# Three mixer parts of 256, 256 and 512 tokens, one token tile moved between the dense and the gathered expert pass, and 1-KB gate runs

## The chip, the cores and the metric

The kernel runs on one core of one Trainium2 chip. The metric is the device time of one execution in microseconds (us). Five engines work side by side: TensorE (PE, with its weight loads shown apart as PEld), VectorE (DVE), ScalarE (ACT), GpSimd (POOL, which issues the indirect DMAs) and SyncE (SP, which issues most other DMAs). All DMAs share 16 DMA engines.

## The reference

One layer of a decoder, 1024 tokens of width 1024, all in float32:

```python
h = rms_norm(x, norm_mix_g);  proj = h @ w_in
x = x + concat([diff_attention(...), mlstm(...)]) @ w_out        # the mixer, causal
# PEER: per token 8 heads x 16 experts out of 16384
xb = rms_norm(x, norm_ffn_g)
q = xb @ w_query;  s = einsum(q, sub_keys)                       # 2 x 128 scores per head
eidx, top_s = product_top_k(top_k(s, 16))                        # second top-k, 16 of 256 sums
g = softmax(top_s)
a = gelu(einsum('td,thkd->thk', xb, expert_u[eidx]))
x = x + einsum('thk,thkd->td', g * a, expert_v[eidx])
x = x + sigmoid(rms_norm(x, norm_ple_g) @ w_ple_gate) * (p @ w_ple_proj)
out = rms_norm(x, final_norm_g)
```

## The kernel before

The 1024 tokens are eight tiles of 128. A float32 product is made of three fp32r matmuls (high by high, high by low, low by high), so each weight block is split on the chip into a high half (ACT) and a low half (DVE). PE issues these from `mm3s`, line L143.

**Front** (`front(part, ptk)`, L220). It runs twice, for tiles 0 to 3 and 4 to 7 (T = 512 columns, NT = 4 tiles). Each part streams 29 blocks of `w_in` (4 heads of 7, and the gates), 8 of `w_out` and 16 of `w_query`, each 512 KB, through `weight` (L190: DMA, ACT L195, DVE L196; three raw buffers, two split ones). A block of `w_in` or `w_query` feeds 24 matmuls of N = T columns. Around them lie attention, mLSTM, the norm, and the first top-k (L595 to L604).

**Experts.** Tiles 4 to 7 (`DORD`, 512 tokens) go the dense way, tiles 0 to 3 (`NS` = 4) the sparse way.
- `dense_up` (L818): for each of 128 blocks j of `expert_u`, load and split it (`table`, L753 and L754), 24 matmuls of N = 512 against the normed activations that the second part left in SBUF, Gelu into `ga` (L866), and a store to DRAM `ga_s`. Beside it `gate_blocks` (L764) spreads the chosen softmax weights into a dense gate table in DRAM, `g_s`, in 32 pieces (PE L806, L807). The second top-k of the part run last is called from here (`late`).
- `dense_down` (L879): for each of 128 blocks of `expert_v`, split it (L753, L754 again), multiply `ga` by the gate (L915), split (L916, L917) and 24 matmuls of N = 512 into eight PSUM banks (`keep`). `gq` (the gate, runs of 4 j x 32 tokens x 4 B = 512 B) and `aq` (the activations) come back from DRAM in groups of GC = 4 blocks.
- `sparse` (L704): one step gathers 128 rows of `expert_u`, one per token (512 KB, L700 into `ru`), dots them with the activations on DVE (L716), gathers 128 rows of `expert_v` (`rv`) and adds them with their weight to `ya` (DVE L734). There are 128 such pairs per tile; the v half runs 16 steps behind. `ring["bufs"]` buffers of each kind are in flight: 4 at first, 8 in `dense_down`, 2 from block FLUSH = 108.

**Order.** The sparse work is a generator. `pump(x)` (L212) adds x to a debt and takes that many steps from it, at a scheduling priority 800 instructions lower; the front pumps only in part 1 (`F_RATE * part`), then `dense_up` at 1.5 and 1.6 steps per block and `dense_down` at 1.6, and `tail` 8 twice per tile. The generator is topk2 of tiles 0 and 1, topk2 of tiles 2 and 3 (14 yields each), then the steps of tiles 0 to 3. Each queue keeps the order fixed at build time. In part 1 the loads of x stand on POOL's queue (L235, L251).

**Tail** (`tail`, L956): per tile the last norm, gate and projection (48 and 12 matmuls of N = 512), in the order 4, 0, 5, 1, 6, 2, 7, 3. For tiles 0 to 3 it first reads `x3_s`, which `sparse` writes when the tile is done (L738, L969).

Of the kernel before, what the change touches and what calls it, by code (L numbers as in the profile page):

```python
# [24 lines left out]
NPART = S // T  # L25
# [13 lines left out]
NS = 4  # L39
NDT = S // P - NS  # L40
TD = NDT * P
DORD = list(range(NT, 2 * NT)) + list(range(NS, NT))
NX = 2 * P if NDT > NT else 0
CH1 = T - (NX - (NDT - NT) * P) if NDT > NT else T
GC = 4
GQB = 2
VBF = 4
# [23 lines left out]
F_RATE = (2.4, 1.6, 2.0)  # L71
UP_RATE = (1.5, 1.6, 56)
DOWN_RATE = 1.6
# [3 lines left out]
def layer(ctx, tc, x, xT, pT, gcols, grows, win, convw, convb, gbias, lams, wout, wq, subk,  # L77
          wple, wproj, eu, ev, ut, vr, ident_d, maskneg_d, maskpos_d, tri_d, sel_d, bl_d, br_d, iota_d, out):
# [18 lines left out]
    gcol = load_const(gcols, [P, 21], "gcol")  # L97
    ident = const.tile([P, P], F32, name="ident")
# [8 lines left out]
    ga_s = dram.tile([P, P, TD], F32, name="ga_s")  # L107
# [38 lines left out]
    def bcast_rows(pool, psum, cols, name):  # L146
        ps = psum.tile([P, NT, P], F32, name="tr")
        for i in range(NT):
            pe.matmul(ps[:, i, :], cols[:, i:i + 1].to_broadcast([P, P]), ident,
                      start=True, stop=True)  # L150
        r = pool.tile([P, T], F32, name=name)
# [3 lines left out]
    eidx, gsm, sel_i, fcs = {}, {}, {}, {}  # L155
# [64 lines left out]
    def front(part, ptk):  # L220
        t0 = part * NT
        with ExitStack() as c1:
# [5 lines left out]
            with pool(f"pa{part}", bufs=1) as pa:  # L228
# [3 lines left out]
                for dc in range(DC):  # L232
                    if dc % 2 == 0:
                        x2t = pa.tile([P, 2, T], F32, name="p", bufs=3)
                        (gp if part else sy).dma_start(x2t, xT[part, :, dc:dc + 2, :])  # L235
# [21 lines left out]
                def project(blk):  # L257
                    pump(F_RATE[0] * part)
# [71 lines left out]
                for h in range(H):  # L330
# [5 lines left out]
                    if part:  # L336
                        sy.dma_start(kT[:, :T], kt_s[h])
                        sy.dma_start(vv[:, :NT, :], v_s[h])
                    ps = project(h * 7 + 1)
                    v.tensor_tensor(kT[:, part * T:(part + 1) * T], ps, rb, op=OP.mult)  # L340
                    ps = project(h * 7 + 2)
                    by_tile(vv[:, t0:t0 + NT, :], token_major(ps), lambda i: r1[:, i:i + 1])
                    if part < NPART - 1:
                        sy.dma_start(kt_s[h], kT[:, :T])
                        sy.dma_start(v_s[h], vv[:, :NT, :])
# [3 lines left out]
                    for i in range(NT):  # L349
# [39 lines left out]
                        jb = pa.tile([P, P], BF16, name="jb", bufs=2)  # L389
# [95 lines left out]
                    for i in range(NT):  # L485
                        jb = pa.tile([P, P], BF16, name="jb", bufs=2)
# [17 lines left out]
            with pool(f"pb{part}", bufs=1) as pb_:  # L504
# [13 lines left out]
                for blk in range(2):  # L518
                    pss = [sps.tile([P, 2, 512], F32, name="S") for _ in range(2)]
                    for q in range(4):  # L520
                        pump(F_RATE[2] * part)
# [30 lines left out]
                for i in range(NT):  # L552
                    if t0 + i < NS or t0 + i in DORD[CH1 // P:]:
# [15 lines left out]
                for hc in range(2):  # L569
                    pump(F_RATE[1] * part)  # L570
                    pair.append((*weight(wp, wq[hc], [DC, P]), mmp.tile([P, T], F32, name="mm")))
                for cs in (slice(0, T // 2), slice(T // 2, T)):
# [568 lines left out]
```

## Time and profile before

| | us |
|---|---|
| median of 3 runs (3245.26 to 3264.1) | 3249.8 |
| profiled execution | 3289.41 |
| its span, first to last instruction | 3287.6 |
| PE, DVE, ACT, POOL busy in it | 2711.8, 2651.6, 1046.9, 1372.9 |

The span is what the rows describe; the profiled execution's own time holds 1.8 us around it. Busy time of an engine is the union of its instructions; a chain of back-to-back instructions overlaps, so that the distance from start to start is shorter than the duration of one. The number of the mean granted clock is a share of TensorE's 2.4 GHz.

### The profile page before, as it was taken

What the parts mean: (1) busy time and instruction counts of PE and PEld (TensorE: products, weight loads), DVE (VectorE), ACT (ScalarE), POOL (GpSimd) and SP (SyncE); (2) the same over time, 40 slices, a digit from 0 to 9 for tenths busy, and PEclk for the clock granted to TensorE, in tenths of its full rate; (3) what the DMA queues carried; (4) which work ended last, traced back from release to release, by engine and by line L of the source; (5) the groups of instructions that cost most, each with busy time, mean ns of one, the idle gap of its engine ahead of it and who ended that gap; (6) DMA issues with size and microseconds to landing.
All of it is one profiled execution on the core that took longest, in us unless ns stands there. A gap on an engine that the chain in (4) does not pass through costs nothing.

```text
span 3287.6 us, 37409 instructions
## 1 busy us (share of the span) xinstructions
PE 2711.8 (82%) x12348; PEld 2143.1 (65%) x12348; DVE 2651.6 (81%) x5837; ACT 1046.9 (32%) x1755; POOL 1372.9 (42%) x1044
## 2 busy tenths in 40 slices
PE   8999889999989986999899996878888887827602
PEld 6777766576777765787787875666666666615401
DVE  5555697788899999887998987778888787998863
ACT  4445333344422323343344432222222222203200
POOL 0000000133332554655565674465555556674561
PEclk9999997799999996999999998989998988968856
DMA  3113431355674987999999999999999999997873
GB/s 137 65 63 107 143 120 38 119 188 183 237 260 151 350 311 272 380 377 371 366 412 367 413 408 370 351 371 352 359 360 362 339 383 371 389 336 271 265 258 119
DMA packets 326467, 911.85 MB, mean 277 GB/s; under 512 B 28480, under 2 KB 101056, under 8 KB 324224
## 3 DMA queue, kind: packets, MB, share of 16 engines
q0 software_dynamic: 149760, 545.33, 45.0%
q1 hardware_dynamic: 158080, 330.57, 27.9%
q10 hardware_dynamic: 18432, 33.56, 2.7%
q8 instruction: 97, 1.59, 0.2%
q14 instruction: 98, 0.80, 0.1%
HBM read 827.56 MB, written 81.79 MB: 277 GB/s over the span
## 4 chain that ended last, share of the span: by engine, by line
PE 37%; DMA 20%; DVE 18%; issue 16%; POOL 7%; ACT 2%; DVEq 0%; POOLq 0%; SPq 0%; ACTq 0%
PE mm L143 13%; PE A L143 9%; DMA raw<-in_vr 7%; DMA ru<-in_eu,eidx 5%; DMA rv<-in_ev,eidx 5%; DVE ya L734 4%; POOL rv L700 3%; POOL ru L700 3%; PE S L359 3%; DVE ru L716 3%; PE S L143 2%; DVE tlo L754 2%; PE tr L387 1%; PE pg L807 1%; PE pg L806 1%
## 5 line engine op out<-in xcount | busy, mean ns | idle before, releaser
L700 POOL DMA_INDIRECT ru<-in_eu,eidx x512 | 673.2, 1315 | 869.8 <-DVE ru L716 441.3
L700 POOL DMA_INDIRECT rv<-in_ev,eidx x512 | 690.6, 1349 | 507.9 <-DVE ya L734 304.0
L734 DVE SCALAR_TENSOR_TENSOR ya<-rv,cf,ya 128x1024 f32<-128x1024 f32 x512 | 657.0, 1283 | 101.7 <-DMA rv<-in_ev,eidx 78.6
L716 DVE SCALAR_TENSOR_TENSOR ru<-ru,sh 128x1024 f32<-128x1024 f32 x512 | 624.1, 1220 | 41.9 <-DMA ru<-in_eu,eidx 37.1
L753 ACT ACTIVATE thi<-raw 128x1024 fp32r<-128x1024 f32 x256 | 271.5, 1061 | 921.4 <-DMA raw<-in_vr 510.3
L143 PE MATMUL A<-ahi,thi 128*128 128x512 f32 x1024 | 408.0, 398 | 11.7 <-ACT ga L866 6.4
L754 DVE TENSOR_TENSOR tlo<-raw,thi 128x1024 fp32r<-128x1024 f32 x256 | 312.3, 1220 | 122.0 <-ACT thi L753 112.0
L143 PE MATMUL A<-alo,thi 128*128 128x512 f32 x1024 | 404.2, 395 | 0.0
L143 PE MATMUL keep<-thi,ph 128*128 128x512 f32 x1024 | 284.3, 424 | 144.6 <-ACT ph L916 75.7
L143 PEld LDWEIGHTS keep<-thi,ph 128*128 128x128 f32 x1024 | 207.4, 205 | 201.3 <-ACT ph L916 81.1
L143 PE MATMUL mm<-ahi,whi 128*128 128x512 f32 (+1 forms) x752 | 302.1, 406 | 17.4 <-ACT ahi L237 9.2
L143 PE MATMUL mm<-alo,whi 128*128 128x512 f32 (+1 forms) x752 | 292.5, 402 | 6.7 <-DVE alo L238 6.7
L143 PE MATMUL keep<-tlo,ph 128*128 128x512 f32 x1024 | 267.8, 406 | 20.4 <-DVE tlo L754 20.1
L143 PE MATMUL A<-ahi,tlo 128*128 128x512 f32 x1024 | 263.9, 401 | 23.9 <-DVE tlo L754 23.8
L143 PE MATMUL keep<-thi,pl 128*128 128x512 f32 x1024 | 256.9, 394 | 6.3 <-DVE pl L917 6.3
L143 PEld LDWEIGHTS keep<-tlo,ph 128*128 128x128 f32 x1024 | 203.6, 200 | 68.5 <-DVE tlo L754 23.7
L143 PEld LDWEIGHTS A<-ahi,tlo 128*128 128x128 f32 x1024 | 196.3, 193 | 70.5 <-DVE tlo L754 29.7
L143 PEld LDWEIGHTS A<-ahi,thi 128*128 128x128 f32 x1024 | 195.7, 191 | 57.9 <-ACT ga L866 12.1
L143 PEld LDWEIGHTS keep<-thi,pl 128*128 128x128 f32 x1024 | 195.0, 191 | 47.9 <-DVE pl L917 6.7
L143 PEld LDWEIGHTS A<-alo,thi 128*128 128x128 f32 x1024 | 195.6, 191 | 39.5
L143 PE MATMUL mm<-ahi,wlo 128*128 128x512 f32 (+1 forms) x752 | 196.0, 391 | 2.8 <-DVE wlo L196 2.8
L196 DVE TENSOR_TENSOR wlo<-wraw,whi 128x1024 fp32r<-128x1024 f32 x106 | 129.1, 1218 | 58.7 <-ACT whi L195 44.1
(436 smaller groups left out, 4149.2 us busy)
## 6 DMA issues: line engine op xcount, KB each, us to landing
raw<-in_ut SPq DMA_DIRECT2D x128, 512.0 KB, 7.0
raw<-in_vr SPq DMA_DIRECT2D x128, 512.0 KB, 7.8
ga_s<-ga ACTq DMA_DIRECT2D x128, 256.0 KB, 6.6
g_s<-st SPq DMA_DIRECT2D x16, 2048.0 KB, 10.4
gq<-g_s SPq DMA_DIRECT2D x32, 1024.0 KB, 9.9
aq<-ga_s SPq DMA_DIRECT2D x32, 1024.0 KB, 12.2
wraw<-in_win SPq DMA_DIRECT2D x58, 512.0 KB, 3.4
wraw<-in_wq SPq DMA_DIRECT2D x32, 512.0 KB, 4.1
```

The lines of the kernel that those rows point to most:

```text
L143: pe.matmul(o, ll if p == "l" else lh, rl if p == "r" else rh, start=start and p == "h", stop=stop and n == last and p == names[-1])
L196: anchor(v.tensor_sub(lo.rearrange("p a b -> p (a b)"), raw, hi.rearrange("p a b -> p (a b)").bitcast(F32)))
L359: pe.matmul(sp_[:, n0:n1], qT[64 * c:64 * c + 64, i * P:(i + 1) * P], kT[64 * c:64 * c + 64, n0:n1], start=True, stop=False)
L387: pe.matmul(po, wT[:, kt, :], vv[:, kt, :], start=kt == 0, stop=kt == g)
L700: gp.indirect_dma_start(out=b, out_offset=None, in_=table, in_offset=bass.IndirectOffsetOnAxis(ap=eidx[part][:, i, k:k + 1], axis=0))
L716: behind(v.scalar_tensor_tensor(b, b, 1.0, st["h", tl], op0=OP.mult, op1=OP.mult, accum_out=st["d", n][:, j:j + 1]))
L734: op = v.scalar_tensor_tensor(ya, b, st["c", n][:, j:j + 1], ya, op0=OP.mult, op1=OP.add)
L753: sc.activation(hi, raw, AF.Copy)
L754: anchor(v.tensor_sub(lo, raw, hi.bitcast(F32)))
L806: pe.matmul(pg[:, b, :], o0[:, a, :, b], w0[:, a, :, b], start=True, stop=False)
L807: pe.matmul(pg[:, b, :], o0[:, a, :, b], w1[:, a, :, b], start=False, stop=True)
```

## The change

The front runs three times: tiles 0 and 1, tiles 2 and 3 (256 columns each), tiles 4 to 7 (512). Every part streams all 53 weight blocks. The generator starts after the first part: topk2 of tiles 0 and 1, sparse of tiles 0 and 1, topk2 of tiles 2 and 3, sparse of tile 2. Tile 3 leaves `sparse`. It joins tiles 4 to 7 in `dense_up`, which now works on 640 columns (384 of the part in SBUF, and 256 of tiles 7 and 3 that are loaded from `h2_s` and transposed), and its activations go to `ga_s` with rows of 640. In `dense_down` the new generator `middle` fetches tile 3's 128 chosen activations per token out of `ga_s`, one number per token by an indirect DMA, multiplies them by the softmax weights, gathers the rows of `expert_v` and adds them up. `gq` is loaded for GQ = 8 blocks at a time (runs of 8 x 32 x 4 B = 1 KB). The pump rates differ.

```diff
-NPART = S // T
+PARTS = ((0, 2), (2, 2), (4, 4))
+NPART = len(PARTS)
-NS = 4
-NDT = S // P - NS
+NS = 3
+DORD = list(range(NT, 2 * NT))
+MID = [3]
+UORD = DORD + MID
+NDT = len(DORD)
 TD = NDT * P
+TU = len(UORD) * P
+NX = 2 * P
+CH1 = TU - NX
+GQ = 8
-F_RATE = (2.4, 1.6, 2.0)
-UP_RATE = (1.5, 1.6, 56)
-DOWN_RATE = 1.6
+F_RATE = ((0.0, 0.0, 0.0), (1.0, 0.8, 1.0), (2.4, 1.6, 2.0))
+UP_RATE = (1.8, 2.0, 56)
+DOWN_RATE = 1.05
...
-    ga_s = dram.tile([P, P, TD], F32, name="ga_s")
+    ga_s = dram.tile([P, P, TU], F32, name="ga_s")
...
     def front(part, ptk):
-        t0 = part * NT
+        t0, NT = PARTS[part]
+        T = NT * P
...
-                        jb = pa.tile([P, P], BF16, name="jb", bufs=2)
+                        jb = pa.tile([P, P], BF16, name="jb", bufs=1)
...
-                    if t0 + i < NS or t0 + i in DORD[CH1 // P:]:
+                    if t0 + i < NS or t0 + i in UORD[CH1 // P:]:
...
+            for n, tl in enumerate(UORD):
+                if tl in MID and t0 + tg <= tl < t0 + tg + TG:
+                    i = tl - t0
+                    aidx[tl] = sp.tile([P, PH * K], I32, name=f"aidx{tl}")
+                    own[tl] = sp.tile([P, PH * K], F32, name=f"own{tl}")
+                    v.scalar_tensor_tensor(own[tl], i1a[:, i, :], 128.0, i0a[:, i, :], op0=OP.mult, op1=OP.add)
+                    v.tensor_scalar(aidx[tl], own[tl], float(TU), colp[:, n:n + 1], op0=OP.mult, op1=OP.add)
...
+    def middle(tiles, rs):
+        flat = ga_s.rearrange("j i t -> (j i t)")[:, None]
+        units = [(tl, k0) for tl in tiles for k0 in range(0, PH * K, K)]
+        ya = {}
+
+        def value(n, j):
+            tl, k = units[n][0], units[n][1] + j
+            gp.indirect_dma_start(out=own[tl][:, k:k + 1], out_offset=None, in_=flat,
+                                  in_offset=bass.IndirectOffsetOnAxis(ap=aidx[tl][:, k:k + 1], axis=0))
+
+        for n in range(len(units) + 1):
+            if n > 0:
+                tl, k0 = units[n - 1]
+                part, i = LOC[tl]
+                cf = rs.tile([P, K], F32, name="cf", bufs=2)
+                v.tensor_tensor(cf, own[tl][:, k0:k0 + K], gsm[part][:, i, k0:k0 + K], op=OP.mult)
+                if k0 == 0:
+                    ya[tl] = rs.tile([P, D], F32, name="ya", bufs=1)
+                    gp.dma_start(ya[tl], x2_s[tl])
+            for j in range(K):
+                if n < len(units):
+                    value(n, j)
+                if n > 0:
+                    b = gather(k0 + j, tl, ev, "ru" if j % 2 else "rv")
+                    behind(v.scalar_tensor_tensor(ya[tl], b, cf[:, j:j + 1], ya[tl], op0=OP.mult, op1=OP.add))
+                    if j % 2 == 0:
+                        continue
+                yield True
+            if n > 0 and k0 + K == PH * K:
+                sy.dma_start(x3_s[tl], ya[tl])
+                stored.add(tl)
...
-            it = gp_.tile([P, 4, P], F16, name="it", bufs=2)
+            it = gp_.tile([P, 4, P], F16, name="it", bufs=1)
...
-            late = chain(lambda: topk2(1, ptk, [0, 2]))
+            late = chain(lambda: topk2(2, ptk, [0, 2]))
...
-                    gq, aq = gtiles(g0 // GC)
-                    sy.dma_start(gq, g_s[:, :, g0:g0 + GC, :].rearrange("b i j t -> i b (j t)"))
-                    sy.dma_start(aq, ga_s[g0:g0 + GC].rearrange("j i t -> i j t"))
+                    if g0 % GQ == 0:
+                        gq = mp.tile([P, P // GB * NDT, GQ, GB], F32, name="gq", bufs=GQB)
+                        sy.dma_start(gq, g_s[:, :, g0:g0 + GQ, :].rearrange("b i j t -> i b (j t)"))
+                    aq = gtiles(g0 // GC)
+                    sy.dma_start(aq, ga_s[g0:g0 + GC, :, :TD].rearrange("j i t -> i j t"))
...
-    pumped["gen"] = chain(lambda: topk2(0, ptk, [0]), lambda: topk2(0, ptk, [2]),
-                          lambda: sparse(range(NS), rs))
-    front(1, ptk)
+    pumped["gen"] = chain(lambda: topk2(0, ptk, [0]), lambda: sparse(range(2), rs), lambda: topk2(1, ptk, [0]),
+                          lambda: sparse(range(2, NS), rs))
+    for part in range(1, NPART):
+        front(part, ptk)
...
+    pumped["gen"] = chain(*([lambda g=pumped["gen"]: g] if pumped["gen"] else []), lambda: middle(MID, rs))
     dense_down(yac)
```

## Rows read from the trace of the kernel before

**Rows 1.** The page: the span, the busy time of each engine, and the span in 40 slices (tenths busy, granted clock in tenths, DMA share in tenths, GB/s).

```profile
span 3287.6 us, 37409 instructions
PE 2711.8 (82%) x12348; PEld 2143.1 (65%) x12348; DVE 2651.6 (81%) x5837; ACT 1046.9 (32%) x1755; POOL 1372.9 (42%) x1044
PE   8999889999989986999899996878888887827602
DVE  5555697788899999887998987778888787998863
PEclk9999997799999996999999998989998988968856
DMA  3113431355674987999999999999999999997873
```

**Rows 2.** Busy time by stretch (windows): length of the stretch, busy us (instructions) of each engine, granted clock, DMA share, GB/s. The stretches are front part 0, front part 1, the first 31 blocks of dense_up, the rest of it, dense_down, and the tail; their bounds are in rows 3.

```profile
0.00:470.00 470.00, 435.95 (x2169) 340.82 (x2169) 291.88 (x1182) 210.00 (x480) 3.04 (x9) 0.97 0.29 101
470.00:1048.00 578.00, 540.37 (x2447) 391.58 (x2447) 495.02 (x1772) 223.16 (x486) 144.75 (x120) 0.89 0.50 169
1048.00:1300.00 252.00, 204.64 (x927) 164.50 (x928) 250.31 (x732) 78.44 (x94) 127.39 (x93) 0.88 0.83 303
1300.00:1977.00 677.00, 642.82 (x3190) 535.71 (x3189) 593.66 (x677) 266.67 (x309) 406.66 (x294) 0.97 0.98 384
1977.00:2897.00 920.00, 752.37 (x3072) 606.04 (x3072) 732.77 (x940) 206.78 (x269) 498.37 (x377) 0.91 0.99 364
2897.00:3288.00 391.00, 135.62 (x544) 104.46 (x544) 288.01 (x539) 61.88 (x119) 192.71 (x154) 0.66 0.72 244
```

**Rows 3.** Single lines of the program within front part 0, front part 1, or the whole span: count, shortest, median and longest duration in ns, start of the first and of the last one. L586 is the end of a query block (16 per part), L333 the first use of a head's first projection (4 per part), L866 the Gelu of dense_up, L929 the first work after dense_down.

```profile
L586 ACT ACTIVATE qq<-mm x16: 597/598/600, 368.8 to 464.5; 128x512 f32<-128x512 f32 x16
L333 DVE SCALAR_TENSOR_TENSOR qT<-mm,rb x4: 676/682/686, 497.0 to 786.6; 128x512 f32<-128x512 f32 x4
L586 ACT ACTIVATE qq<-mm x16: 597/598/602, 947.1 to 1047.9; 128x512 f32<-128x512 f32 x16
L866 ACT ACTIVATE ga<-A x128: 575/598/648, 1060.6 to 1977.3; 128x512 f32<-128x512 f32 x128
L929 DVE TENSOR_TENSOR yac<-keep,yac x8: 674/674/679, 2896.6 to 2901.9; 128x512 f32<-128x512 f32 x8
```

**Rows 4.** The timeline of PE: start, length, what. Two of 16 matmuls of 256 columns that follow one another, two of 16 of 512 columns, and two of 30 gate matmuls.

```profile
365.77 0.28 PE L143 MATMUL mm<-ahi,whi 128*128 128x256 f32 x1
...
367.54 0.28 PE L143 MATMUL mm<-ahi,wlo 128*128 128x256 f32 x1
...
1718.58 0.39 PE L143 MATMUL A<-ahi,thi 128*128 128x512 f32 x1
...
1721.98 0.39 PE L143 MATMUL A<-alo,thi 128*128 128x512 f32 x1
...
1724.03 0.29 PE L806 MATMUL pg<-w,o 128*128 128x128 f16 x1
...
1727.45 0.30 PE L807 MATMUL pg<-w,o 128*128 128x128 f16 x1
```

**Rows 5.** The same stretches for line L716 alone, the dot of a sparse step: two instructions (the product and the reading of its sum) per step.

```profile
470.00:1048.00 578.00, 76.02 (x124) 0.89 0.50 169
1048.00:1300.00 252.00, 56.14 (x92) 0.88 0.83 303
1300.00:1977.00 677.00, 181.79 (x295) 0.97 0.98 384
1977.00:2897.00 920.00, 220.82 (x362) 0.91 0.99 364
2897.00:3288.00 391.00, 93.48 (x152) 0.66 0.72 244
```

**Rows 6.** The timeline of DVE where steps follow one another without a wait.

```profile
2910.78 1.24 DVE L716 SCALAR_TENSOR_TENSOR ru<-ru,sh 128x1024 f32<-128x1024 f32 x1
...
2913.18 1.21 DVE L716 SCALAR_TENSOR_TENSOR ru<-ru,sh 128x1024 f32<-128x1024 f32 x1
```

**Rows 7.** DMA queues in the stretch 1300 to 1977, and the stores of the activations: packets, MB, share of 16 engines (q0 is what POOL issues, q1 SP, q10 ACT); for an issue its count, KB each, us to landing.

```profile
q0 software_dynamic: 42404, 154.41, 58.6%
q1 hardware_dynamic: 16091, 79.83, 29.3%
q10 hardware_dynamic: 13968, 25.43, 9.9%
ga_s<-ga ACTq DMA_DIRECT2D x97, 256.0 KB, 6.7
```

**Rows 8.** The same for the stretch 1977 to 2897.

```profile
q0 software_dynamic: 54034, 196.74, 55.5%
q1 hardware_dynamic: 101989, 137.25, 43.4%
ru<-in_eu,eidx POOLq DMA_INDIRECT x187, 8.9
rv<-in_ev,eidx POOLq DMA_INDIRECT x186, 8.9
```

**Rows 9.** Who waited for whom, over the whole span: us in total, times, longest.

```profile
ACT thi L753 <- DMA raw<-in_vr: 510.3, 106, 20.1
POOL ru L700 <- DVE ru L716: 441.3, 128, 21.8
PE tr L984 <- DMA x<-x_s: 146.6, 1, 146.6
```

**Rows 10.** The weight stream of the front, from the page: the low half's split, and the loads (KB each, us to landing).

```profile
L196 DVE TENSOR_TENSOR wlo<-wraw,whi 128x1024 fp32r<-128x1024 f32 x106 | 129.1, 1218 | 58.7 <-ACT whi L195 44.1
wraw<-in_win SPq DMA_DIRECT2D x58, 512.0 KB, 3.4
```

**Rows 11.** The end of the timeline: the last store of a sparse tile, its reload, and the first and one of the last instructions that use it.

```profile
3253.21 0.33 SPq L738 DMA_DIRECT2D x_s<-ya  x1
3255.88 0.33 SPq L969 DMA_DIRECT2D x<-x_s  x1
3259.10 1.97 PE L984 MATMUL tr<-ident,x 128*128 128x128 f32 x8 [146.60 <-DMA x<-x_s]
...
3275.97 1.27 ACT L1017 ACTIVATE gt<-acc,hr 128x512 f32<-128x512 f32 x2 [4.41 <-PE acc L143]
```

**Rows 12.** The slice of the front with the lowest granted clock among windows of 80 us, columns as in rows 2.

```profile
480.00:560.00 80.00, 77.09 (x274) 46.34 (x274) 57.38 (x318) 29.91 (x59) 1.05 (x2) 0.76 0.17 56
```

More of the change, by code (lines that the diff above doesn't have):

```diff
@@ L24 @@
 NT = T // P
-NPART = S // T
+PARTS = ((0, 2), (2, 2), (4, 4))
+NPART = len(PARTS)
+LOC = {t0 + i: (n, i) for n, (t0, nt) in enumerate(PARTS) for i in range(nt)}
 DC = D // P
@@ L146, in bcast_rows @@
     def bcast_rows(pool, psum, cols, name):
-        ps = psum.tile([P, NT, P], F32, name="tr")
-        for i in range(NT):
+        nt = cols.shape[-1]
+        ps = psum.tile([P, nt, P], F32, name="tr")
+        for i in range(nt):
             pe.matmul(ps[:, i, :], cols[:, i:i + 1].to_broadcast([P, P]), ident,
                       start=True, stop=True)
-        r = pool.tile([P, T], F32, name=name)
+        r = pool.tile([P, nt * P], F32, name=name)
         sc.activation(r, ps.rearrange("p a b -> p (a b)"), AF.Copy)
         return r
-    eidx, gsm, sel_i, fcs = {}, {}, {}, {}
+    eidx, gsm, sel_i, fcs, aidx = {}, {}, {}, {}, {}
+    own = {}
     def front_consts(fc):
@@ L220, in front @@
     def front(part, ptk):
-        t0 = part * NT
+        t0, NT = PARTS[part]
+        T = NT * P
+        xT_ = xT[:, t0 * DC * P:(t0 + NT) * DC * P].rearrange("p (c t) -> p c t", c=DC)
+        f_rate = F_RATE[part]
         with ExitStack() as c1:
@@ L518, in front @@
                 for blk in range(2):
-                    pss = [sps.tile([P, 2, 512], F32, name="S") for _ in range(2)]
+                    pss = [sps.tile([P, 2, 512], F32, name="S") for _ in range(NT // 2)]
                     for q in range(4):
-                        pump(F_RATE[2] * part)
+                        pump(f_rate[2])
                         hi, lo = weight(wp, wout[blk, q], [2, 512])
@@ L569, in front @@
                 for hc in range(2):
-                    pump(F_RATE[1] * part)
+                    pump(f_rate[1])
                     pair.append((*weight(wp, wq[hc], [DC, P]), mmp.tile([P, T], F32, name="mm")))
-                for cs in (slice(0, T // 2), slice(T // 2, T)):
+                for cs in (slice(0, T // 2), slice(T // 2, T)) if T > 256 else (slice(0, T),):
                     for a in pair:
@@ L580, in front @@
                     else:
-                        pump(F_RATE[1] * part)
+                        pump(f_rate[1])
                         hi, lo = weight(wp, wq[hc], [DC, P])
@@ L608, in topk2 @@
         sv, sfa = fcs["sv", part]
-        t0 = part * NT
+        t0, NT = PARTS[part]
         if part in gsm:
@@ L615, in topk2 @@
         sel_i[part], gsm[part] = (i0a, i1a), gsa
-        if t0 < NS:
+        if t0 < NS or any(t0 <= tl < t0 + NT for tl in MID):
             eidx[part] = sp.tile([P, NT, PH * K], I32, name=f"eidx{part}")
@@ L621, in topk2b @@
         sv, sfa = fcs["sv", part]
-        t0 = part * NT
+        t0, NT = PARTS[part]
         i0a, i1a = sel_i[part]
@@ L720, in coef @@
             tl, k0 = units[n]
-            part, i = divmod(tl, NT)
+            part, i = LOC[tl]
             cf = rs.tile([P, K], F32, name="cf", bufs=2)
@@ L770, in gate_blocks @@
         for n, tl in enumerate(DORD):
-            part, i = divmod(tl, NT)
+            part, i = LOC[tl]
             fl = gp_.tile([P, 3, P], F32, name="fl", bufs=1)
@@ L963, in tail @@
             for tl in TORD:
-                part, i = divmod(tl, NT)
-                if tl < NS:
+                part, i = LOC[tl]
+                if tl not in DORD:
                     while tl not in stored:
@@ L1113, in layouts @@
         iota_d=np.arange(P, dtype=f),
+        colp_d=np.arange(TU, dtype=f).reshape(len(UORD), P).T,
         ident_d=np.eye(P, dtype=f),
```

46 lines of the change are left out of this document (22 added, 24 removed).

## The prediction

> **What bounds the kernel now.** I read the page first [rows 1]: no engine is above 82% over the span, and the digits change from stretch to stretch, so the average says nothing. The DMA digits are 1 to 5 in the first third and 9 from slice 19 to 36; PE falls to 0 near the end. Then the windows by stage [rows 2], cut at the ends of the stages [rows 3].
> - Front part 0, 470 us: PE 436 busy at clock 0.97, DVE 292, DMA 0.29. PE is the bound and nothing is gathered.
> - Front part 1, 578 us: PE 540, DVE 495.
> - dense_up: first 252 us DVE, 250 busy. Then 677 us in which PE is 643 busy and DMA 0.98: the two are about even.
> - dense_down, 920 us: DMA 0.99, PE 752. The split of the table waits 510 us for its raw block [rows 9], so DMA is the bound.
> - Tail, 391 us: PE works 136. It waits 147 us in one piece for the last sparse tile [rows 9], which is stored at 3253 and reloaded [rows 11].
>
> So transfers are short of room late and have plenty early, and the sparse tiles are finished too late.
>
> **Prices.** From start to start [rows 4], 15 intervals each: a matmul of 256 columns takes 1.77 / 15 = 0.118 us, of 512 columns 3.40 / 15 = 0.227; a gate matmul 3.42 / 29 = 0.118. No matmul of 384 columns is in the trace: it lies between 0.118 and 0.227, and I take the middle, 0.172, because the two rows grow with the columns. A sparse step (u and v) takes DVE 2913.18 - 2910.78 = 2.40 us [rows 6]. A gather takes all DMA engines 0.555 x 920 / 373 = 1.37 us [rows 8].
>
> **Front, parts 0 and 1: 470 becomes 590.** Before, 45 blocks of `w_in` and `w_query` and 8 of `w_out` give 53 x 24 x 0.227 = 288 us of L143; the other 182 are small matmuls and chains. Two half parts: 2 x 45 x 24 x 0.118 = 255, `w_out` 44 (its columns are weights, so its count halves with the tiles), together 299; the 182 divide over the tiles. New: a second start, from the last query block to the first head, 497.0 - 464.5 = 32 us [rows 3]. Weight supply: a half-width block gives PE only 24 x 0.118 = 2.83 us, while its raw block lands in 3.4 and its low half takes DVE 1.22 [rows 10]. Two split and three raw buffers hide most of it. The bounds are 0 and 3.4 + 1.22 - 2.83 = 1.8 us per block, that is 0 to 190 us over 106 blocks; I take 0.45, 47 us, since buffers overlap the loads. Part 1 pumps 49.8 yields (29 x 1.0 + 8 x 1.0 + 16 x 0.8), of which some 25 run there: 25 x 2.4 = 60 us of DVE, beside a DVE that was busy 62% in part 0; half on the path, 30 (0 to 60). Sum 299 + 182 + 32 + 47 + 30 = 590.
>
> **Part 2: 578 becomes 592.** Its 28 yields of second top-k are gone (one pair of tiles is now in part 1, one in dense_up). Before, 83 steps were pumped (111 yields less 28) and 124 / 2 = 62 ran [rows 5], 21 behind. After, 161 - 14 = 147 are pumped by its end; 21 behind is 126, some 20 of them in part 1. DVE: 495, less 54 pairs x 2.4 = 130, less at most 73 for the top-k (495 - 292 - 130), plus 106 x 2.4 = 254, is 546. PE's 540 stays, so both are near full: 592 (578 to 640). The loads of x for this part now stand behind gathers on POOL's queue; its longest wait for a ring buffer is 22 us [rows 9], so 0 to 22, which is inside that range.
>
> **dense_up: 929 becomes 1120.** PE per block: 24 x (0.172 + 0.118) = 6.97 against 5.44. The second stretch holds 97 blocks [rows 7]; PE's floor there was 97 x 5.44 + 873 x 0.118 (L806, L807) = 631 of 677, 93%. After: 97 x 6.97 + 103 = 779, over 0.93 = 838. The first stretch is DVE's: 0.3 more steps in 31 blocks, 22 us, on 252, plus the transposes of the two reloaded tiles (16, under 10 us): 282. Together 1120. Others beside it: DMA was 0.83 x 252 + 0.98 x 677 = 873 us. Steps run: 378 - 126 = 252, less the half-filled ends, 470 gathers against 385 [rows 2, 5], so + 116, and the wider `ga_s` rows add a quarter of 0.099 x 677 = 67, 17: 1006 of 1120. DVE: 844, plus 58 more steps and one more top-k (14 yields) at 2.4, 173: 1017. All three are near full. The ends are PE's floor, 128 x 6.97 + 122 = 1014, and all at the first stretch's pace, 1190.
>
> **dense_down: 920 becomes 760.** After dense_up 38 sparse steps are left, some 64 gathers, and `middle` adds 128 of `expert_v`: 192 x 1.37 = 263 us against 511. The rest of its DMA was 0.434 x 920 = 399. Runs of 512 B are slower: q1 moved 137 MB at 0.434 here and 80 MB at 0.293 x 677 in the stretch without `gq`, that is 21.5 against 25.2 bytes per ns and engine. All of the 59 us that this costs is the most that longer runs can give back; half the number of runs, I take 25. The 128 small gathers move a thousandth of the bytes: I take 10, between 0 and a full gather's 175. Sum 263 + 374 + 10 = 647. PE's floor 128 x 5.44 = 696, over 0.93 = 748, plus 12 for the first load, which is now twice as long: 760. PE becomes the bound here; with the small gathers at their upper end DMA would be (812, at 0.99 about 820). `cf` waits on DVE for sixteen small gathers, and the split of the next table block queues behind it. They are issued a unit ahead, so nothing; without that lead, eight landings of 8.9 us [rows 8], 71.
>
> **Tail: 391 becomes 160.** `middle` needs 80 yields after those 38; 1.05 x 128 = 134 are pumped. At the end of dense_down before, 459 were pumped and 436 run. A lag of 23 leaves some 8 yields for the tail, and tile 3 is last in its order. PE's work: 384 + 96 matmuls x 0.227 and 64 transposes, together 125; the first evacuation 5, the chain after the last gate 12 [rows 11], and 18 for the six weight blocks still to be split: 160 (140 to 200).
>
> **At nothing:** `jb` and `it` with one buffer are written and read in order by one engine (ACT, DVE), and no wait in the trace names them; if DVE and ACT were apart there, 0.4 us x 32. The extra `h2` store goes to SP behind the weight loads, once.
>
> **Sum.** 590 + 592 + 1120 + 760 + 160 = 3222 against 470 + 578 + 929 + 920 + 391 = 3288, with 1.8 around it 3224 against the profiled 3289.41. The median stands at 3249.8 / 3289.41 = 0.988 of that execution: **3185**.
>
> **The rivals.**
> - **Half-width blocks starve PE (slower).** If weights come late in parts 0 and 1, PE idles between blocks and its granted clock falls, as in the slice after the start of part 1: 0.76, between the levels of 2.4 and 1.2 GHz [rows 12]. The 481 us of PE's path then become 481 x 0.97 / 0.76 = 614: + 133, 3355 in the span, 3315. It decides against the change from 66 us on, a mean clock of 0.85. For it: 2.83 us of work under a 3.4-us load. Against it: part 0 holds 0.97 at an unbroken stream, and three raw buffers.
>  The Trainium skill (TensorE: Matmul & The Clock Gate, "HAM oscillation — how this bites in real kernels") warns of just this: where a tile's matmuls are shorter than the wait for the next load, the clock drops in every tile. Taken in full, at 1.2 GHz throughout both parts, that would be an estimate of some 3630; the trace has no slice of 80 us in the front below 0.76, so it bears out only the milder form.
> - **The backlog runs in the front (no change).** If the 21 steps that I leave behind run within part 2's query blocks, they cost 21 x 2.4 = 50 us there, and dense_up, bound by PE, gives nothing back: 3235.
> - **It doesn't start earlier.** The scheduler may leave the pumped steps of parts 1 and 2 behind, as it did with a quarter of them: with 80 done instead of 126, 92 gathers move on, 126 us of DMA, of which dense_up (114 free) and dense_down (113 free) take most; some 40 stay: 3225.
> - **Larger gain.** Parts 0 and 1 at 512 (no stall), dense_up at 1070 and dense_down at 730: 158 us less, half of it at once likely: 3105.
>
> **How the numbers follow.** Forecast 0.53, starving 0.21, backlog 0.12, no earlier start 0.05, larger gain 0.09. A difference below about 0.5% can't be told from no change here. Faster than 3234: most of the forecast and all of the last, part of the middle ones, 0.62; within 0.5%: 0.16; slower: the first rival and a little more, 0.22. The range reaches to the larger gain and to the milder starving: 3090 to 3310; the forecast's own is 3120 to 3240.
>
> **What would show it.** Right: last query block of the second part near 590 and of the third near 1180 at a clock of 0.9 or more; matmuls of 384 columns 0.17 us apart; dense_up about 1120 long with PE over 90% busy; in dense_down no long waits for `in_vr`; no wait of the tail for `x3_s`; tile 3's store before the tail's last tile. Wrong: a clock near 0.76 before 590, a dense_up beyond 1190, or a tail that still waits.

## The result, and the profile after

The changed kernel takes **3299.21 us** (median of 4 runs, 3294.1 to 3300.06) against 3253.53 (4 runs, 3245.26 to 3264.1) for the kernel before on the same chip: a ratio of 1.0124, 95% interval 1.0096 to 1.0151. It is slower by 1.2%. The prediction was 3185, faster; the measured time lies inside its range of 3090 to 3310, on the wrong side.

Where did the time go? First the page after, its span and some of its digits [rows 1].

```profile
span 3298.0 us, 46190 instructions
PE   7988977699997969988999899999597799989998
DVE  5678889877888989999898878998575467777655
PEclk8899998788998979999999999999798899999999
DMA  4253386865668579889999589999987688988521
```

The empty end is gone: PE reads 9 where it fell to 0. The DMA row is higher early and is no longer 9 late. So what the change was to move did move. The windows by stage of the kernel after, columns as in [rows 2], cut at the same instructions as before (here the stages are parts 0, 1 and 2, dense_up, dense_down, tail):

```profile
0.00:278.00 278.00, 243.38 (x1577) 216.51 (x1577) 184.38 (x701) 135.07 (x310) 3.08 (x9) 0.90 0.43 143
278.00:582.00 304.00, 247.88 (x1628) 212.19 (x1628) 266.43 (x1011) 141.18 (x312) 55.78 (x49) 0.91 0.57 196
582.00:1197.00 615.00, 542.13 (x2452) 399.94 (x2452) 525.18 (x1448) 232.73 (x498) 256.83 (x203) 0.88 0.69 235
1197.00:2332.00 1135.00, 1055.74 (x7205) 1043.60 (x7204) 1002.64 (x1776) 373.23 (x542) 652.21 (x484) 0.95 0.90 348
2332.00:3160.00 828.00, 722.55 (x3067) 591.13 (x3068) 536.77 (x605) 209.18 (x266) 383.45 (x306) 0.93 0.80 287
3160.00:3298.00 138.00, 121.88 (x551) 98.68 (x549) 83.90 (x282) 55.73 (x106) 0.00 (x0) 0.96 0.19 67
```

The profiled execution of before was a long one: 3289.41 against a median of 3249.8. For a fair ledger I took a second profile of the same kernel (first of the experiments below), whose execution took 3247.51, near the median. Its windows:

```profile
0.00:464.00 464.00, 431.56 (x2160) 336.78 (x2160) 287.39 (x1156) 204.70 (x471) 3.05 (x9) 0.98 0.29 102
464.00:1023.00 559.00, 517.64 (x2457) 381.52 (x2456) 498.32 (x1800) 227.83 (x493) 144.92 (x120) 0.94 0.51 175
...
1949.00:2856.00 907.00, 751.57 (x3072) 604.63 (x3072) 732.80 (x940) 206.91 (x269) 500.51 (x377) 0.92 1.00 369
2856.00:3246.00 390.00, 133.84 (x544) 103.03 (x544) 288.21 (x539) 61.82 (x119) 191.79 (x154) 0.68 0.72 245
```

| stage, us | predicted | before, 1st profile | before, 2nd | after | after - 2nd |
|---|---|---|---|---|---|
| parts ahead of the last | 590 | 465 | 464 | 582 | +118 |
| last part | 592 | 583 | 559 | 615 | +56 |
| dense_up | 1120 | 929 | 926 | 1135 | +209 |
| dense_down | 760 | 920 | 907 | 828 | -79 |
| tail | 160 | 391 | 390 | 138 | -252 |
| span | 3222 | 3288 | 3246 | 3298 | +52 |

383 us are paid in the front and in the first pass, 331 come back. The trade is of the predicted kind; the prices were a little off, and dense_down gave back half of what it should (79 of 160).

In dense_down of the kernel after, who waited for whom (us in total, times, longest):

```profile
ACT thi L804 <- DMA raw<-in_vr: 453.3, 87, 24.3
POOL rv L719 <- DVE ya L794: 147.5, 29, 51.1
PE keep L150 <- ACT thi L804: 70.0, 10, 35.1
DVE aq L967 <- DMA aq<-ga_s: 65.2, 15, 26.9
DVE ya L753 <- DMA rv<-in_ev,eidx: 59.7, 11, 23.0
```

DMA is only 0.80 busy and PE 722.55 of 828, so neither is full, and yet the split of the table still waits 453 us for its block, with a longest wait longer than before [rows 9]: one of the signs that the prediction named, "no long waits for `in_vr`", did not come. Two suspects stand in the rows of the same stretch, the gate load of 2 MB (KB each, us to landing) and the 128 small gathers (ns; first and last start):

```profile
raw<-in_vr SPq DMA_DIRECT2D x128, 512.0 KB, 5.8
gq<-g_s SPq DMA_DIRECT2D x15, 2048.0 KB, 16.3
```

```profile
L777 POOL DMA_INDIRECT own<-ga_s,aidx x128: 941/948/1992, 2352.6 to 2624.0; - x128
```

A block of the second pass wants 5.44 us of PE, and a gate load now takes three times that to land. And all 128 small gathers were issued within 271 us, long before tile 3 needs the last of them, with the row gathers of tile 2 behind them on the same queue.

### The profile page after: what moved, and what is told of

Its sections match the earlier page's. It is cut to its first block, busy times and chain, and to the rows that moved or that the text cites. A ratio compares the mean times of both kernels' runs of the same rounds, so it can differ in the third digit from the quotient of the medians.

```text
span 3298.0 us, 46190 instructions
## 1 busy us (share of the span) xinstructions
PE 2933.6 (89%) x16476; PEld 2562.0 (78%) x16476; DVE 2599.3 (79%) x5819; ACT 1147.1 (35%) x2033; POOL 1351.4 (41%) x1049
## 4 chain that ended last, share of the span: by engine, by line
PE 48%; DVE 17%; DMA 16%; issue 10%; POOL 6%; ACT 3%; SPq 0%; DVEq 0%; POOLq 0%; ACTq 0%
PE A L150 13%; PE mm L150 10%; PE keep L150 9%; DMA rv<-in_ev,eidx 4%; DMA raw<-in_vr 3%; DMA ru<-in_eu,eidx 3%; DMA aq<-ga_s 3%; PE acc L150 2%; PE S L371 2%; POOL own L777 2%; POOL ru L719 2%; DVE ya L753 2%; DVE ya L794 2%; DVE ru L735 2%; PE S L150 2%
## 5 line engine op out<-in xcount | busy, mean ns | idle before, releaser
L150 PE MATMUL mm<-ahi,whi 128*128 128x256 f32 (+1 forms) x1096 | 347.2, 339 | 45.3 <-ACT ahi L249 28.3
L150 PE MATMUL A<-ahi,thi 128*128 128x384 f32 x1024 | 354.3, 346 | 5.1 <-ACT ga L917 2.6
L150 PE MATMUL A<-alo,thi 128*128 128x384 f32 x1024 | 350.2, 342 | 0.0
L150 PE MATMUL mm<-alo,whi 128*128 128x256 f32 (+1 forms) x1096 | 335.2, 334 | 3.7 <-DVE alo L250 3.7
L150 PEld LDWEIGHTS mm<-ahi,whi 128*128 128x128 f32 x1096 | 222.2, 203 | 60.6 <-ACT ahi L249 29.2
L150 PE MATMUL A<-xh,thi 128*128 128x256 f32 x1024 | 251.3, 283 | 0.7 <-ACT xh L896 0.7
L150 PE MATMUL A<-xl,thi 128*128 128x256 f32 x1024 | 251.7, 283 | 0.0
L150 PE MATMUL mm<-ahi,wlo 128*128 128x256 f32 (+1 forms) x1096 | 217.5, 331 | 19.9 <-DVE wlo L205 19.2
L150 PEld LDWEIGHTS mm<-alo,whi 128*128 128x128 f32 x1096 | 217.8, 202 | 18.3 <-DVE alo L250 5.1
L150 PE MATMUL A<-ahi,tlo 128*128 128x384 f32 x1024 | 206.7, 344 | 24.1 <-DVE tlo L805 24.0
```

The lines of the kernel that those rows point to most:

```text
L150: pe.matmul(o, ll if p == "l" else lh, rl if p == "r" else rh, start=start and p == "h", stop=stop and n == last and p == names[-1])
```

## The experiments

Theories after the result: **burst** (one gate load of 2 MB per eight blocks holds up the table's blocks) against **queue** (the small gathers hold up the row gathers), and later **the same wait is bought twice** (the three parts and tile 3's new mode both remove the tail's wait, and each is paid for). Diffs are against the changed kernel unless told otherwise. "Late" values means that the small gathers are tied into the order of the table's subtractions, as the sparse steps are. The columns are stages in us of each run's profile (front: to the end of the last part); ratios are to the kernel before on the same chip, and the runs were spread over several chips, so that kernels of different chips are compared by their ratios too.

| run | parts | gate blocks | values | front | up | down | tail | median us | ratio (95%) |
|---|---|---|---|---|---|---|---|---|---|
| b_again | 2 | 4 | none | 1023 | 926 | 907 | 390 | 3247.51, one run | |
| b_gq8 | 2 | 8 | none | 1034 | 925 | 958 | 388 | 3297.61 | 1.0117 (1.0082 to 1.0151) |
| a_gq4 | 3 | 4 | early | 1201 | 1144 | 843 | 138 | 3325.79 | 1.0203 (1.0159 to 1.0247) |
| a_spread | 3 | 8 | late | 1190 | 1142 | 800 | 137 | 3276.39 | 1.0075 (1.0056 to 1.0095) |
| a_noval | 3 | 8 | left out | 1198 | 1138 | 793 | 138 | 3269.62, one run | |
| a_split | 3 | 8, two loads | late | 1192 | 1144 | 792 | 139 | 3268.39 | 1.0014 (0.9975 to 1.0053) |
| a_gq4_spread | 3 | 4 | late | 1197 | 1138 | 790 | 138 | 3262.06 | 1.0014 (0.9986 to 1.0043) |
| parts_only | 3 | 4 | none | 1187 | 930 | 920 | 243 | 3291.89 | 1.0116 (1.0031 to 1.0200) |
| two_parts | 2 | 4 | late | 1031 | 1145 | 890 | 138 | 3196.19 | 0.9793 (0.9715 to 0.9872) |
| two_parts_early | 2 | 4 | early | 1025 | 1145 | 892 | 138 | 3199.51 | 0.9836 (0.9813 to 0.9859) |
| two_parts_gq8 | 2 | 8 | late | 1030 | 1149 | 904 | 138 | 3213.84 | 0.9886 (0.9848 to 0.9925) |
| quiet3 | 3 | 4 | late | 1154 | 1104 | 801 | 301 | 3371.38 | 1.0354 (1.0298 to 1.0411) |
| quiet2 | 2 | 4 | late | 1047 | 1105 | 883 | 272 | 3299.63 | 1.0098 (1.0061 to 1.0134) |

**The kernel before, once more.** No edit.

> The kernel before once more, for one profile that can be set beside the first. If its first profiled execution was an ordinary one, span again near 3288 with stages 465, 583, 929, 919 and 391. If that execution was one of the long ones, span near 3253 and one of the stages some 35 us shorter; the factor of 0.988 in the prediction was then a property of one execution and not of every kernel.

The span is 3245.8, 42 us shorter than in the first profile: 24 of it in front part 1 (clock 0.94 against 0.89 [rows 2]) and 13 in dense_down. So the first profile was of a long execution of this kernel, and its excess is no factor that belongs to every kernel.

**Gate runs alone**, one at a time in each kernel.

```diff
-GQ = 8
+GQ = 4        (a_gq4; in b_gq8 the reverse, in the kernel before)
```

> The kernel before with only the gate loaded for 8 blocks at a time (runs of 1 KB, 2 MB per load). By the term in the prediction (25 us of DMA time given back in a dense_down that DMA bounds, 0 to 59): dense_down falls from 920 to 880-910, but the tail still waits for the last sparse tile, so that only part shows: median 3225-3250. Burst theory: the 2-MB loads cost as much as or more than they save, dense_down 910-980, median 3250-3310. Queue theory says nothing of it.

> The changed kernel with the gate loaded for 4 blocks at a time again (runs of 512 B, 1 MB per load); all else as changed. Burst theory (the 2-MB gate load stands ahead of the table blocks and costs PE some 8 us in every second group of four blocks): dense_down falls from 828 us to 740-770, the 7.2 to 7.9 us per block of every second group go to 5.4-6.2, the median falls from 3299 to 3220-3250. Queue theory (the 128 small gathers hold up the row gathers on POOL's queue): dense_down stays at 820-850, the two groups above 10 us per block between 2500 and 2640 stay, the median is 3290-3325, slightly worse by the slower runs.

b_gq8 is what the burst theory wants: +1.2%, with dense_down 51 us longer than in the second profile of before. Its queues (packets, MB, share of 16 engines) and its longest-waited-for transfer in dense_down, and below them the same lines of the second profile of before:

```profile
q0 software_dynamic: 53969, 196.53, 53.9%
q1 hardware_dynamic: 68636, 136.78, 39.9%
ACT thi L754 <- DMA raw<-in_vr: 605.3, 113, 27.4
```

```profile
q0 software_dynamic: 54014, 196.66, 56.0%
q1 hardware_dynamic: 101687, 137.09, 44.0%
ACT thi L753 <- DMA raw<-in_vr: 484.9, 106, 20.1
```

The loads of longer runs did save transfer time: q1 moves the same bytes in a third fewer packets and in 0.399 x 958 = 382 us where it took 0.440 x 907 = 399. But DMA is now 94% busy where it was 100%, and the table's waits grew by 120 us. 17 us of transfer were won and 51 of the stage lost. The Trainium skill (DMA: Bandwidth & Descriptors, section "Bandwidth") advises to batch transfers to 1 MiB or more. The gate load of four blocks has that size already; from there to 2 MB the transfer still gained and the stage lost. The same page ("Queues, rings and completion order") says that each DMA engine takes the descriptors of one ring in order. Gate and table loads are issued on the same queue, so that a table block behind a long gate load would wait for it; the longer waits agree with that and don't prove it.

a_gq4 should have won back as much, and was slower still: its dense_down of 843 lies where the queue theory had it, its median of 3326 just above. But it has a stall that no other run has to this extent; it is told under the unexpected below.

**The small gathers.** Later in POOL's order, or left out:

```diff
-            gp.indirect_dma_start(out=own[tl][:, k:k + 1], ...)
+            behind(gp.indirect_dma_start(out=own[tl][:, k:k + 1], ...))   # a_spread; in a_noval none is issued
```

> The changed kernel with each small gather held back, in the build's order only, behind the newest table split, so that the row gathers of tile 2 come first on POOL's queue. Queue theory: dense_down falls by 30-70 us (760-800), DVE no longer waits 9 to 23 us for rv of tile 2, the median is 3230-3270. Burst theory: only the part of the two worst groups goes, 10-25 us; the pattern of every second group stays; the median is 3275-3295.

> The changed kernel without the 128 small gathers (left out: the fetch of tile 3's activations, so that its rows are added with wrong weights). Queue theory: dense_down 740-770, span near 3220-3240. Burst theory: dense_down 795-815, every second group still 7.2 to 7.9 us per block, span 3265-3285.

dense_down falls from 828 to 800 and 793, the median by 23 us in a_spread. Neither theory has all the numbers: a_spread's stage is at the edge of the queue theory's and its median is the burst theory's, and a_noval lies close to the burst theory's (793 for 795 to 815). What the queue theory said of the wait did come: between 2340 and 2700 VectorE waits for tile 2's rows in the kernel after (first line) and no longer in a_spread (second).

```profile
DVE ya L753 <- DMA rv<-in_ev,eidx: 58.3, 9, 23.0
DVE ya L753 <- DMA rv<-in_ev,eidx: 0.9, 1, 0.9
```

So the place of the small gathers in the queue costs some 30 us of the stage, and the transfers themselves, the difference between late and none, hardly anything (7 us, one profile each). In a_noval every second group of four blocks between 2740 and 2980 still took 6.9 to 8.2 us a block for 5.4: the other part is not the queue's.

**Both out, and the load cut in two.** a_gq4_spread joins the two edits above; a_split has the small gathers late and keeps the runs of 1 KB, but issues each 2-MB load as two of 1 MB, half a group apart, while the group before it is worked on.

```diff
-                    if g0 % GQ == 0:
-                        sy.dma_start(gq, g_s[:, :, g0:g0 + GQ, :]...)
...
+                    if g0 + GQ < P:
+                        gate_load(g0 // GQ + 1, g0 % GQ // GC)     # one half of its blocks
```

> The changed kernel with both suspected costs out: the gate runs back at four blocks (512-byte runs, 1 MB a load) and the small value gathers later in POOL's order. If the two costs add: the pattern in every second group is gone and no group is over 7 us a block, dense_down 745 to 770 us, span 3215 to 3225, median 3215 to 3235, about 1% under the kernel before. If the stall of TensorE's own queue seen with four-block gates comes back (it is then not bound to the small gathers): dense_down 820 or more, median 3300 or more.

> The small gathers later, the 1-KB gate runs kept, but each 2-MB load cut in two loads of 1 MB with 1-KB runs, issued half a group apart. Burst theory (one 2-MB load stands ahead of the table block's loads): the pattern is gone, dense_down 740 to 770, median 3210 to 3235. If a group of eight blocks itself is the cause, whatever the size of its loads: dense_down 790 to 800 as with the small gathers later alone, median near 3276.

Of the two sums neither came. The strict alternation goes, but single groups still take up to 8.4 us a block in a_gq4_spread and 8.0 in a_split, and dense_down stops at 790 and 792, above the 770 that both allowed. a_split's 792 is what its second expectation had, that a group of eight is the cause whatever the size of its loads; but with groups of four it is 790, so that isn't shown either. Cutting the load took 8 us off a_spread's median and stage (by the ratios, 1.0075 and 1.0014, it is nearer 20). What the record does show: from block 64 on, the stage takes 50 us more than 5.4 per block in the kernel after, 56 in a_spread, 48 in a_noval, 41 in a_split and 51 in a_gq4_spread. Neither edit touches this part, and its cause is open; a_gq4 alone, after its stall, has 7 there. Both kernels are level with before. dense_down in a_gq4_spread, and the first and last start of its table matmuls of one kind:

```profile
2335.00:2680.00 345.00, 305.97 (x1318) 250.85 (x1319) 223.54 (x269) 93.69 (x118) 139.77 (x111) 0.94 0.88 314
2680.00:3125.00 445.00, 410.16 (x1751) 332.22 (x1750) 314.14 (x337) 116.17 (x148) 231.51 (x196) 0.97 0.81 291
```

```profile
L150 PE MATMUL keep<-thi,ph x1024: 387/389/797, 2366.2 to 3122.1; 128*128 128x512 f32 x171
```

dense_up ends at 2335, so the first matmul comes 32 us later (35 in the kernel after, 24 in both profiles of before). From there the stage takes 790 - 32 = 758 us, and the prediction had 748: with both edits in, the stage's length is near the forecast one, and 20 us of the rest are the start. That is partly luck: the forecast's 52 us over PE's floor of 696 were a share taken over from dense_up, and here they sit mostly in the slow groups from block 64 on.

**One half of the change at a time.** parts_only has the three parts, with tile 3 gathered in both passes as before; two_parts has tile 3's new mode with the two old parts.

```diff
-PARTS = ((0, 2), (2, 2), (4, 4))
-DOWN_RATE = 1.05
+PARTS = ((0, 4), (4, 4))
+DOWN_RATE = 1.3                                  (two_parts; F_RATE and the order of the generator as before)
...
-NS = 3
-MID = [3]
+NS = 4
+MID = []                                         (parts_only, with the rates of before behind the front)
...
```

> Only the three-part split: token tile 3 gathered in both passes as before, four-block gates. The front ends near 1200 (150 later than before), the first pass takes 930, dense_down 910 to 920; if the earlier start of the gathers takes the tail's waits, the tail is 140 to 200 and the span 3190 to 3240. Rival, the tail still waits for its rows: tail near 390 less a little, span 3300 or more.

> The three-part split undone (two parts of 512), four-block gates, the small gathers later; token tile 3 stays dense in the first pass and gathered in the second. If the head start of the gathers is not what matters: the first two mixer parts end near 1048 (150 us earlier than with three parts), the first pass 1130, dense_down 790 to 830, tail 140: span 3110 to 3150. Rival, the head start is needed: dense_down 900 or more with waits for gathered rows, or a tail that waits, span 3220 or more.

This is the main finding. **two_parts is 2.1% faster than before** (1.3 to 2.9), and **parts_only is 1.2% slower** (0.3 to 2.0). Against the second profile of before, two_parts pays 219 us in dense_up and 8 in the front and gets 252 in the tail and 17 in dense_down: its tail is the same 138 as with three parts. Its second front part and its tail:

```profile
463.00:1031.00 568.00, 524.38 (x2456) 384.05 (x2456) 498.49 (x1799) 230.04 (x495) 147.42 (x120) 0.92 0.51 175
3065.00:3203.00 138.00, 121.72 (x553) 97.71 (x551) 84.09 (x282) 55.61 (x106) 0.00 (x0) 0.97 0.18 65
```

parts_only pays 164 in the front and gets 147 in the tail; there the tail still stops for rows (its window, and two waits in it):

```profile
3037.00:3280.00 243.00, 129.87 (x544) 101.42 (x544) 192.88 (x421) 61.26 (x117) 104.39 (x79) 0.77 0.67 231
```

```profile
PE acc L150 <- ACT hg L994: 46.3, 3, 39.5
PE tr L1036 <- DMA x<-x_s: 32.0, 1, 32.0
```

Each half aims at the same 250 us. Tile 3's mode buys all of them; with it in place the three parts cost 166 us of front and get back 100 in dense_down (890 to 790) and 7 in dense_up: a_gq4_spread is 59 us of span and 66 us of median behind two_parts. Both kernels came out between what their two expectations had: two_parts with a dense_down of 890 (790 to 830, or 900 and more) and a span of 3203 (3110 to 3150, or 3220 and more), parts_only with a tail of 243 (140 to 200, or near 390) and a span of 3280. One rival is untested: the pump rates went with the halves (those of before in parts_only, 1.8, 2.0 and 1.3 in two_parts), and no run has the kernel before with higher rates. Against it speaks that VectorE was busy 250 of 252 us in the first stretch of dense_up and DMA 0.98 and 0.99 after it [rows 2], so that there was little room for more steps.

**Are the two small costs there without the three parts?** In two_parts, GQ = 8 (two_parts_gq8), or the small gathers early again (two_parts_early).

> Two mixer parts, tile 3 dense then gathered, small gathers later, and only the gate runs put back to eight blocks (1-KB runs, 2 MB a load), as in the changed kernel. If the 2-MB load costs whatever the front is: some 40 us over the 3196 of the two-part kernel, so 3225 to 3245, all of it in dense_down. If it costs only where little else is outstanding (14 us between the three-part kernels with and without it): 3196 to 3215.

> Two mixer parts, four-block gates, and only the small value gathers put back to where the program writes them, without the order that holds them behind the table's subtractions. If their place in POOL's order is a cost by itself: they run back to back and hold the row gathers, 25 to 60 us over 3196, so 3220 to 3255, in dense_down. If they cost only together with three parts: 3190 to 3205.

Eight gate blocks cost 18 us of median here, 14 of it in dense_down, just inside the second expectation; that it is the size of the load is not shown, since PE's waits of the kind told in the last section rise with it, from 26 us to 54. The place of the small gathers costs nothing that can be told (3 us, the intervals overlap). Why it costs some 30 us with three parts and nothing here, no run shows.

**Why the last part is longer.** Before it took 583 and 559 us; in the seven kernels with three parts and these rates it took 605 to 619. The pump's rates there cut to half or less, in a_gq4_spread (quiet3) and in two_parts (quiet2):

```diff
-F_RATE = (..., (1.0, 0.8, 1.0), (2.4, 1.6, 2.0))
+F_RATE = (..., (1.0, 0.8, 1.0), (1.0, 0.7, 0.9))     (quiet3; quiet2: two_parts with (1.2, 0.8, 1.0))
```

> Three parts, four-block gates, small gathers later, and the sparse steps pumped in the third part at the second part's rate (1.0, 0.7, 0.9 for 2.4, 1.6, 2.0), so that more than half of that part's gathers move behind it. If the steps that run in the third part are what makes it 608 us where two parts take 560 to 568: it ends 25 to 45 us earlier, 565 to 585 us long. If the part is longer for another reason (its weights or its start): 600 to 610. The moved steps come back later: dense_up is near TensorE's floor, dense_down 20 to 100 us longer, so 3240 to 3320 in all.

> Two parts, with the second part's sparse steps at half the rate. If steps in the front cost it about half a step's time on VectorE each: the second part 540 to 555 us where it was 560 to 568, and dense_down longer by more than that: 3200 to 3240. If they are free there: 560 to 568 still, and 3210 to 3250.

The last part in a_gq4_spread and in quiet3:

```profile
589.00:1197.00 608.00, 534.04 (x2452) 395.13 (x2452) 525.50 (x1449) 233.31 (x499) 256.79 (x203) 0.89 0.69 238
```

```profile
582.00:1154.00 572.00, 515.58 (x2452) 383.16 (x2452) 426.75 (x1318) 230.34 (x494) 138.24 (x110) 0.93 0.49 168
```

PE's instructions are the same; with 99 us less on DVE (and DMA at 0.49 for 0.69) the part is 36 us shorter, as expected if the steps cost it, and well outside the 605 to 619 of the seven profiles. With two parts it doesn't come again: in quiet2 DVE had 74 us less, and the part took 583 instead of 568, at a clock of 0.88 for 0.92, the upper end of the 559 to 583 that two parts took elsewhere. So with three parts the steps are shown to lengthen the part, by one profile, and with two parts not. Both totals are misses: 3371 for 3240 to 3320, and 3300 for 3200 to 3250. dense_down hardly grew in quiet3 (790 to 801) and not in quiet2; what both expectations left out is the tail, which grew to 301 and 272 us. At these rates, what isn't pumped in the front is done last.

## Why the prediction was wrong

The gap closes with four terms: the span came out 3298 for 3222, of which dense_down is 68, the last part 23, dense_up 15, and parts 0 and 1 and the tail gave back 30 together, so 76; the last step took off another 39. 76 + 39 = 115, and 3299 - 3185 = 114.

- **"The median stands at 3249.8 / 3289.41 = 0.988 of that execution": failed.** This step took one long execution's excess and granted it to a kernel that had none: the profiled execution after took 3300.06, at its median of 3299.21. The second profile of before shows that 37 of the 42 us of excess sat in front part 1 and dense_down. Without the factor the forecast would have been 3224, still faster, by 0.9%.
- **"dense_down: 920 becomes 760": failed, 828.** The gathers' sum held: 263 us against 0.317 x 828 = 262 measured. The rest was to fall from 399 to 374 and measured 0.482 x 828 = 399 (queue shares in the fence below, with 3% more bytes than before [rows 8]). Three things failed. "Half the number of runs, I take 25" had the right sign for the transfers in b_gq8 (17) and the wrong one for the stage (51 longer); in this kernel it costs some 10 us of the stage (a_spread 800, a_gq4_spread 790). The small gathers, "a unit ahead, so nothing": ahead of their use they were, but the question of who stands behind them on POOL was not asked: the row gathers do, VectorE waits for them with the table's split behind it, and that costs 28 us of the stage by a_spread. And "12 for the first load" was put on PE's floor without the 24 us that the start took before as well; the start took 35. With a_gq4_spread the 68 us are 28 for the small gathers, 10 for the gate loads, 20 for the start and 10 for the pace. In the first two the price was put on the bytes; for the small gathers the order is shown to be the cost, for the gate loads the cause is open.

```profile
q1 hardware_dynamic: 70334, 141.31, 48.2%
q0 software_dynamic: 30296, 95.45, 31.7%
```

- **"Part 2: 578 becomes 592": mis-sized, 615.** Its range was 578 to 640. The counts were right: 124 steps had run by its end for the 126 forecast, so that the backlog rival's condition was not met; PE was busy 542 us for 540 and DVE 525 for 546. What failed is "both are near full": PE stood idle for 73 us and DVE for 90, where 592 left 52 and 46. Against an ordinary execution of before, the last part's price is 56, not 14. By quiet3, 36 us for 46 steps fewer, the 35 steps more than before [rows 5] are worth 27 of them, an estimate; the other half is open.
- **Parts 0 and 1, 590: right, 582.** The terms cost together what was said; only the second start stands alone in the trace, 303.0 - 277.5 = 25.5 us for 32. The clock there was 0.90 and 0.91 for 0.97 [rows 2], far from the 0.76 of the starving rival and above the mean of 0.85 from which it was to decide. So that rival's direction, slower, came true by another mechanism; nor was its example one of idling, since PE was busy 77 of those 80 us [rows 12]. The Trainium skill (TensorE: Matmul & The Clock Gate, "HAM oscillation — how this bites in real kernels") has the clock fall anew in every tile whose matmuls are shorter than the wait for the next load. Here the lowest slice of 80 us up to 560 is at 0.83, so it does not show in full.
- **dense_up, 1120: right, 1135.** A matmul of 384 columns, between the two rows that were there [rows 4], takes (1697.12 - 1694.51) / 15 = 0.174 us from start to start, and 0.172 was taken. (The upper end is a slip: all blocks at the first stretch's pace are 282 / 31 x 128 = 1164, not 1190. The measured time lies below both.) From the timeline of PE after, two of 16 that follow one another:

```profile
1694.51 0.34 PE L150 MATMUL A<-ahi,thi 128*128 128x384 f32 x1
...
1697.12 0.33 PE L150 MATMUL A<-alo,thi 128*128 128x384 f32 x1
```

- **Tail, 160: right, 138.** No wait for a sparse tile is left; tile 3 was stored at 3075.7, before the tail began.
- **What no step asked.** The prediction added the two halves of the change into one ledger and never asked which half earns the tail's 231 us. Row by row its own numbers say it: three parts cost 590 + 592 - 470 - 578 = 134 us, and dense_down and the tail had to pay for that and for tile 3's 191 together. two_parts shows that tile 3's half pays alone, and a_gq4_spread that the three parts on top of it lose 59 us of span.

One reading of the rows was off as well: the DMA digits are 9 from slice 17 on, not 19, and reach 7 in the first third [rows 1]. No term uses them.

What stays open: how eight gate blocks a load cost the kernel before 51 us of dense_down, what the slow groups from block 64 on wait for, and half of the last part's 56 us.

## What to carry to other kernels

When a change has two halves that both go at the same wait, price each half alone, with the wait credited to one of them only: the second pays again and finds nothing left. Bytes alone don't price a larger or earlier transfer; ask what is queued behind it: here small gathers that move next to nothing cost 28 us by their place in a queue, and 17 us of transfer time won went with 51 us of the stage lost, for a cause that is open. And before a profile's sum is scaled to a median, look at whether the profiled execution is an ordinary one; a factor from one long execution is worth as much as a term of the sum (39 us here).

## What was not expected of the hardware

In a_gq4, with four-block gates and the small gathers back to back on POOL, all engines but POOL nearly stop for some 95 us. Its windows (columns as in [rows 2]) and PE's wait in the second of them:

```profile
2500.00:2545.00 45.00, 35.93 (x112) 24.24 (x111) 21.74 (x23) 8.00 (x10) 35.25 (x33) 0.74 0.78 275
2545.00:2640.00 95.00, 28.79 (x54) 14.33 (x53) 10.60 (x13) 4.43 (x5) 64.38 (x67) 0.54 0.24 75
2640.00:2740.00 100.00, 100.00 (x432) 82.57 (x432) 53.48 (x64) 32.11 (x38) 8.10 (x6) 0.98 0.69 232
```

```profile
PE keep L150 <- issue: 63.8, 37, 3.4
```

54 matmuls run in 95 us, where the next window has 432 in 100; between them PE waits up to 3.4 us for nothing that the profile names, the granted clock is 0.54, near the lower of its two levels (1.2 GHz), DMA is 24% busy, and POOL issues on. It ends with the small gathers, the last of which starts at 2628.6. two_parts_early has a weaker one: 50 matmuls from 2560 to 2600. With the small gathers spread out, a_gq4_spread has no such stretch and is 64 us faster in the median (ratios to before 1.0203 and 1.0014). That gathers in a row bring the long stall about is shown by that pair. Waits of PE for "issue" don't go with it, though: in dense_down they are 72 us in a_gq4, 25 in a_gq4_spread, 28 in a_spread, 11 in a_split and 26 to 54 in two_parts, two_parts_early and two_parts_gq8. In before, b_again, b_gq8, parts_only and a_noval, which issue no small gathers, they are at most 2.1; but the kernel after, quiet2 and quiet3 issue them and have at most 1.5. So the small gathers seem needed for these waits and not enough; through what they bring them about, and why the kernel after has none, is open.
